# Heads' products regrouped (values with the forget gate, queries with z), and keys and values of two blocks turned by VectorE and a trip through DRAM

## The chip, the cores and the metric

The kernel runs on one core of one Trainium2 chip. A core has a matrix engine (TensorE, PE in the profile), a vector engine (VectorE, DVE), an activation engine (ScalarE, ACT), a general engine (GpSimd, POOL) and a synchronising engine (SyncE, SP), each with an instruction stream of its own that it works off in order, and 16 DMA engines that SyncE's and GpSimd's queues feed. The metric is the device time of one execution in microseconds; the kernel before took 2583.63 us, the median of three runs (2581.27 to 2584.62).

## The reference, cut to what matters

One encoder layer over 2048 prompt tokens and 64 sample tokens with 1024 features, in fp32. All projections come from one normed input `h`; the change concerns branch B, a gated linear recurrence over 8 heads with 128 features each, in chunks of 64 tokens:

```
proj = h @ w_in
vA, bA, cA, zA, q, f, iv, zB, gA, gB = split_cols(proj)
fg   = lb + (1 - lb) * sigmoid(f);   logf = log(fg);   k = 1 - fg
q    = silu(q) * 128 ** -0.5;        v = iv
# per chunk, S being the state of the head
b    = cumsum(logf);  ref = b[31]
att  = tril((q * exp(b - ref)) @ (k * exp(ref - b)).T)
o    = att @ v + (q * exp(b)) @ S
S    = exp(b_last) * S + (k * exp(b_last - b)).T @ v
yB   = (rms_norm(o) * g_onorm * silu(zB)) @ w_b_out
```

## The kernel before, in words

**Blocks.** The 2112 tokens (1408 prompt, 64 sample, 640 prompt) run as three blocks of 768, 704 and 640 tokens. Features lie on the partitions, tokens along the free axis. A block goes through branch B (`path_b`, 8 heads one after the other), branch A, the gates, the merge and the output. A block's tokens fall into groups of 128, which are pairs of chunks: six in the first block, five and the sample's lone 64 tokens in the second, five in the third. `bl["parts"]` cuts these into the first four pairs, the remaining pairs, and the lone chunk.

**Products.** Each projection is split into a high and a low fp32r part, three matmuls for one. `sgroup(i1, i2, ...)` makes two projections of the block at once from seven products (Strassen's scheme over two halves of the tokens and of the features) of twelve matmuls each (L442, L443, L444; four steps of k, three parts). The results leave in a fixed order: the first projection's first half at the fifth product, both halves of the second projection at the sixth, the first projection's second half at the seventh (with `free` the very last one goes behind the seventh). A sink takes each piece from PSUM.

**A head.** `head_prep` runs two such groups, forget gate with queries, then z with values. `scaled` runs in the middle of the second group (behind its third product) and makes, on ScalarE and VectorE, the decays `eq`, the scaled keys `kb` (`ka` for the first chunk of a pair) and the head's factors `f`; `queries` scales the queries (`qe`, and `qx` for the state). `sink_v` writes the values `vt`.

**Attention.** `head_attn` is a generator of four steps per part: (1) turn keys and values into tokens on partitions (L1068, L1070, transposes on PE into PSUM, then the copies L1072 and L1073 by ScalarE), then the scores (L1083, L1084) and their mask; (2) the state products (L1098) and the chain of states on VectorE (L1115); (3) the outputs (L1138, L1140) and their norm, whose power runs on GpSimd (L689); (4) turn the outputs back (L1156) and gate them (L1158).

**What sets the order.** Behind every product `hook()` takes the next entry of a list, so a head's attention is worked off between the products of the next head; `path_b` fills the list, step by step, part by part, and the PE instructions of a step are put behind the last product's (`placed()`). `path_b` also puts the store of a head's result (`keep_z`) and the pieces of `lead_sums` into it. A scheduler orders the other engines' streams by dependencies. Weights come through SyncE's queue, other loads and the stores through GpSimd's.

Of the kernel before, what the change touches and what calls it, by code (L numbers as in the profile page):

```python
# [18 lines left out]
P = 128  # L19
# [74 lines left out]
def hybrid_step(  # L94
# [156 lines left out]
    def used_later(idx, part):  # L251
# [5 lines left out]
        if idx in (GB * 8 + KB - 1, QQ * 8):  # L257
            return part != 0
# [677 lines left out]
    def head_prep(bl, hc, hd, first, hs):  # L936
        n, npair = bl["n"], bl["npair"]
        nch, np1 = n // CH, npair * P
        sf, qe = rt(), rt()
        sq = None if first else rt()  # L940

        def sink_f(c, h, x, y):
            if c == 0:
                A.activation(half(sf, h), whole(x, y), AF.Sigmoid)
            else:
                into(half(qe, h), x, y)

        if hs and hd == 0:
            plain_group(FF * 8, QQ * 8, hs, sink_f)
        else:  # L950
            sgroup(FF * 8 + hd, QQ * 8 + hd, hc, sink_f, first)
        if not first:
            A.activation(sq, qe, AF.Sigmoid)
        lg, b, eq = rt(), rt(), rt()
        A.activation(lg, sf, AF.Ln, bias=lb[:, hd : hd + 1], scale=omlb[:, hd : hd + 1])
        if not first:
            V.scalar_tensor_tensor(qe, qe, QK_SCALE, sq, ALU.mult, ALU.mult)
# [6 lines left out]
        ka, kb, qx, vt, z = hf(npair * CH), rt(), rt(), rt(), rt()  # L964

        late = first and hd > 0

        def scaled(after):
# [28 lines left out]
            for lo, hi in ((0, SWAP), (SWAP, npair)):  # L997
                seconds, place = slice(2 * lo + 1, 2 * hi, 2), slice(2 * lo + (hi > SWAP), 2 * hi, 2)
                V.tensor_tensor(chunks(kb)[:, place, :], chunks(sf)[:, seconds, :], chunks(lg)[:, seconds, :], ALU.mult)
            if nch % 2:  # L1000
# [3 lines left out]
            if not late:  # L1004
                queries()

        def queries():
# [3 lines left out]
            else:  # L1011
                V.tensor_tensor(qe, qe, eq, ALU.mult)
            V.tensor_tensor(chunks(qx), chunks(qe), f.unsqueeze(2).to_broadcast([P, nch, CH]), ALU.mult)

        def sink_v(c, h, x, y):
            if c == 1:
                n1 = 0
                if h == 0:
                    n1 = 2 * SWAP * CH
                    for odd in range(2):  # L1020
                        c3, to = (slice(o, 2 * SWAP, 2) for o in (odd, 1 - odd))
                        V.tensor_tensor(chunks(vt)[:, to, :], chunks(x[:, :n1])[:, c3, :], chunks(y[:, :n1])[:, c3, :], ALU.add)
                V.tensor_tensor(half(vt, h)[:, n1:], x[:, n1:], y[:, n1:], ALU.add)
# [7 lines left out]
        with behind_all(summed[-1] if first and hd == 0 else ()):  # L1031
            sgroup(ZB * 8 + hd, IV * 8 + hd, hc, sink_v, first, mid=scaled, free=late)
        if late:
            with tc.issue_after(freed[0]):
                queries()
        return dict(eq=eq, f=f, ka=ka, kb=kb, qe=qe, qx=qx, vt=vt, z=z, more=npair - 2 * SWAP, first=first, last=bl["last"], carry=None)
# [675 lines left out]
```

## Time and profile before

| quantity | value |
|---|---|
| median of 3 runs | 2583.63 us |
| the profiled execution, its own time | 2581.3 us |
| its span in the profile | 2579.6 us |
| PE busy, share of the span | 99% |
| VectorE, ScalarE, GpSimd busy | 67%, 59%, 14% |
| DMA, mean rate over the span | 287 GB/s |
| heads of the second block (1069 to 1350 us), period of a head | 35 us |
| heads of the third block (1870 to 2160 us), period of a head | 31 us |

Busy shares are means over stages; where PE has no gap, its instructions' distance from start to start is what they cost, not the duration of one, since they overlap. A matmul of two full fp32 operands shows as two records, a transpose or an fp32r matmul as one. "us to landing" of a DMA runs from its issue to the arrival of its data.

### The profile page before, as it was taken

The page shows a single profiled execution, that of the slowest core. Times are in us where ns is not written, and L with a number is a line of the kernel's source. Part 1 is how long each engine was busy: PE and PEld are TensorE (multiplying, and loading weights), DVE is VectorE, ACT ScalarE, POOL GpSimd, SP SyncE. Part 2 cuts the span into 40 slices and gives each one's busy share as a digit, 9 for nine tenths or more (in the row PEclk, how much of TensorE's full clock was granted, in tenths as well). Part 3 has the DMA queues.
Part 4 walks back from the last instruction along what each step waited for, and adds up shares of the span by engine and source line. Part 5 has one row for each costly group of instructions (what it writes and reads, how often), then busy time and mean ns, then how long its engine had stood idle before and what let it go on. Part 6 is the DMA issues. An engine that isn't in the chain of part 4 may idle for free.

```text
span 2579.6 us, 47382 instructions
## 1 busy us (share of the span) xinstructions
PE 2562.4 (99%) x16358; PEld 2546.4 (99%) x16358; DVE 1733.2 (67%) x3511; ACT 1529.9 (59%) x2973; POOL 369.5 (14%) x677
## 2 busy tenths in 40 slices
PE   9999999999999999999999999999999999999999
PEld 9999999999999999999999999999999999999998
DVE  7788778898777775466464556987345545336967
ACT  6766676454453764466564555567456665446675
POOL 2011111230022021111111221102100000001011
PEclk9999999999999999999999999999999999999999
DMA  8678777899897898877778998989887788999986
GB/s 327 225 262 289 266 258 272 314 374 304 261 348 241 267 329 264 284 249 233 261 226 290 344 392 312 325 292 338 294 271 246 251 270 265 298 297 324 334 274 201
DMA packets 361233, 739.87 MB, mean 287 GB/s; under 512 B 44118, under 2 KB 48784, under 8 KB 360992
## 3 DMA queue, kind: packets, MB, share of 16 engines
q1 hardware_dynamic: 321696, 582.69, 67.4%
q0 software_dynamic: 39296, 154.14, 16.4%
q8 instruction: 129, 2.11, 0.3%
q14 instruction: 112, 0.92, 0.1%
HBM read 543.44 MB, written 193.22 MB: 286 GB/s over the span
## 4 chain that ended last, share of the span: by engine, by line
PE 86%; issue 5%; DVE 4%; DMA 3%; ACT 1%; POOL 1%; SPq 0%; DVEq 0%; POOLq 0%; ACTq 0%
PE pg L442 18%; PE pg L443 18%; PE pg L444 18%; PE pg L594 4%; PE pg L593 4%; PE pg L595 4%; PE pg L633 3%; PE pg L632 3%; PE pg L631 3%; PE pa L1098 1%; PE pa L1138 1%; PE pa L1140 1%; PE pa L1084 1%; DMA lo<-low 1%; DVE lo L226 1%
## 5 line engine op out<-in xcount | busy, mean ns | idle before, releaser
L442 PE MATMUL pg<-r,hi 128*128 128x320 f32 (+2 forms) x3304 | 1085.2, 328 | 0.6 <-DVE r L490 0.4
L443 PE MATMUL pg<-r,hi 128*128 128x320 f32 (+2 forms) x3304 | 1068.1, 323 | 0.0
L444 PE MATMUL pg<-r,lo 128*128 128x384 f32 (+2 forms) x2356 | 768.7, 326 | 0.9 <-DMA lo<-low 0.9
L273 ACT CAST hi<-raw 128x512 fp32r<-128x512 f32 x730 | 449.6, 620 | 499.7 <-PE pg L443 172.1
L442 PEld LDWEIGHTS pg<-r,hi 128*128 128x128 f32 x3304 | 621.5, 188 | 1.9 <-issue 0.7
L443 PEld LDWEIGHTS pg<-r,hi 128*128 128x128 f32 x3304 | 621.7, 188 | 0.0
L444 PEld LDWEIGHTS pg<-r,lo 128*128 128x128 f32 x2356 | 442.3, 188 | 1.9 <-DMA lo<-low 1.7
L444 PE MATMUL pg<-r,s 128*128 128x352 f32 (+1 forms) x948 | 299.7, 316 | 0.2 <-DMA s<-low 0.2
L594 PE MATMUL pg<-r,hi 128*128 128x320 f32 (+2 forms) x864 | 277.4, 322 | 0.1
L593 PE MATMUL pg<-r,hi 128*128 128x320 f32 (+2 forms) x864 | 275.0, 322 | 0.0
L226 ACT CAST hi<-raw 128x512 fp32r<-128x512 f32 x252 | 155.5, 620 | 155.8 <-PE pg L443 40.0
L226 DVE TENSOR_TENSOR r<-r,r 128x320 fp32r<-128x320 f32 (+7 forms) x354 | 209.5, 611 | 51.9 <-ACT r L226 50.4
L226 ACT CAST r<-r 128x320 fp32r<-128x320 f32 (+7 forms) x354 | 185.8, 557 | 54.4 <-DMA r<-w_blk 10.9
L226 DVE TENSOR_TENSOR lo<-raw,hi 128x512 fp32r<-128x512 f32 x231 | 158.7, 689 | 86.8 <-ACT hi L226 81.5
L595 PE MATMUL pg<-r,lo 128*128 128x352 f32 (+2 forms) x564 | 180.8, 321 | 0.6 <-DMA lo<-low 0.6
L444 PEld LDWEIGHTS pg<-r,s 128*128 128x128 f32 x948 | 177.8, 188 | 0.7 <-DMA s<-low 0.7
L226 ACT CAST hi<-s 128x512 fp32r<-128x512 f32 x156 | 96.3, 618 | 123.9 <-PE pg L443 107.4
L632 PE MATMUL pg<-r,hi 128*128 128x384 f32 (+2 forms) x512 | 167.0, 327 | 0.2 <-DVE r L226 0.2
L631 PE MATMUL pg<-r,hi 128*128 128x384 f32 (+2 forms) x512 | 165.8, 327 | 0.2 <-ACT hi L273 0.2
L594 PEld LDWEIGHTS pg<-r,hi 128*128 128x128 f32 x864 | 162.2, 188 | 2.0 <-DVE r L226 1.4
L593 PEld LDWEIGHTS pg<-r,hi 128*128 128x128 f32 x864 | 161.3, 188 | 1.3 <-ACT r L226 0.7
L456 ACT COPY hf<-pg 128x352 f32<-128x352 f32 (+2 forms) x354 | 157.3, 446 | 1.7 <-PE pg L444 1.3
(403 smaller groups left out, 4110.9 us busy)
## 6 DMA issues: line engine op xcount, KB each, us to landing
raw<-w_blk SPq DMA_DIRECT2D x577, 256.0 KB, 4.1
raw<-S SPq DMA_DIRECT2D x444, 256.0 KB, 4.2
lo<-low SPq DMA_DIRECT2D x422, 256.0 KB, 4.1
s<-low SPq DMA_DIRECT2D x308, 256.0 KB, 4.0
low<-lo SPq DMA_DIRECT2D x271, 256.0 KB, 3.7
S<-s SPq DMA_DIRECT2D x152, 256.0 KB, 3.6
low<-r POOLq DMA_DIRECT2D x54, 256.0 KB, 5.0
r<-w_blk POOLq DMA_DIRECT2D x52, 256.0 KB, 6.6
```

The lines of the kernel that those rows point to most:

```text
L226: return A.copy(hi, src).ins, V.tensor_tensor(lo, src, hi.bitcast(F32), ALU.subtract).ins
L273: A.copy(hi, raw)
L442: add(hi[:, k, :], xhi, start=start and k == 0, stop=False)
L443: add(hi[:, k, :], xlo, start=False, stop=False)
L444: last[0] = add(lo[:, k, :], xhi, start=False, stop=k == KH - 1).ins
L456: copied = A.copy(got[n], ps[bank])
L593: add(hi[:, k, :], xhi, start=start and k == 0, stop=False)
L594: add(hi[:, k, :], xlo, start=False, stop=False)
L595: last[0] = add(lo[:, k, :], xhi, start=False, stop=k == KH - 1).ins
L631: T.matmul(ps, hi[:, k % 4, :], xhi[:, c], start=k == ks[0], stop=False)
L632: T.matmul(ps, hi[:, k % 4, :], xlo[:, c], start=False, stop=False)
L633: last[0] = T.matmul(ps, lo[:, k % 4, :], xhi[:, c], start=False, stop=k == ks[-1]).ins
```

## The change

**The groups of a head.** The first group of a head is now forget gate with values, the second z with queries, so values are there half a head earlier and queries half a head later. `queries` therefore runs behind the second group in all blocks, with the queries' sigmoid in it.

**Turning.** In the second and third block `turned` transposes the 640 columns of the five full groups in blocks of 32 by 32 on VectorE (values into the tile that later holds `qx`, keys into the one that held `b`) and stores the result to DRAM; `in_rows` loads it back in pieces of 160 elements (640 bytes), so that tokens lie on partitions. Keys come back with the five groups interleaved (an element every 20 bytes), values in pieces of 32. PE's transposes and ScalarE's copies of these groups are gone; the lone sample chunk and the whole first block keep them.

**Hooks.** In these blocks a head's steps start two hooks later than the head's list, the full groups' second steps stand in one hook, four behind their first steps, the third steps in one hook, two behind; the sample's steps lie in the hooks between. In the first block one empty hook stands ahead of each head.

```diff
             return part in ("S1", "S2", "S3", "S4")
-        if idx in (GB * 8 + KB - 1, QQ * 8):
+        if idx in (GB * 8 + KB - 1, IV * 8):
             return part != 0
...
         nch, np1 = n // CH, npair * P
-        sf, qe = rt(), rt()
-        sq = None if first else rt()
+        sf, vt = rt(), rt()
...
                 A.activation(half(sf, h), whole(x, y), AF.Sigmoid)
-            else:
-                into(half(qe, h), x, y)
+                return
+            n1 = 0
+            if h == 0:
+                n1 = 2 * SWAP * CH
+                for odd in range(2):
+                    c3, to = (slice(o, 2 * SWAP, 2) for o in (odd, 1 - odd))
+                    into(chunks(vt)[:, to, :], chunks(x[:, :n1])[:, c3, :], None if y is None else chunks(y[:, :n1])[:, c3, :])
+            into(half(vt, h)[:, n1:], x[:, n1:], None if y is None else y[:, n1:])
         if hs and hd == 0:
-            plain_group(FF * 8, QQ * 8, hs, sink_f)
+            plain_group(FF * 8, IV * 8, hs, sink_f)
         else:
-            sgroup(FF * 8 + hd, QQ * 8 + hd, hc, sink_f, first)
-        if not first:
-            A.activation(sq, qe, AF.Sigmoid)
-        lg, b, eq = rt(), rt(), rt()
+            sgroup(FF * 8 + hd, IV * 8 + hd, hc, sink_f, first)
+        lg, b, eq, qx = rt(), rt(), rt(), rt()
+        wrote = None if first else [turned("tv", vt, qx, npair)]
         A.activation(lg, sf, AF.Ln, bias=lb[:, hd : hd + 1], scale=omlb[:, hd : hd + 1])
         if not first:
-            V.scalar_tensor_tensor(qe, qe, QK_SCALE, sq, ALU.mult, ALU.mult)
             V.tensor_scalar(sf, sf, nomlb[:, hd : hd + 1], omlb[:, hd : hd + 1], ALU.mult, ALU.add)
...
         f, r = qc[:, 0, :nch], qc[:, 1, :nch]
-        ka, kb, qx, vt, z = hf(npair * CH), rt(), rt(), rt(), rt()
-        late = first and hd > 0
+        ka, kb, qe, z = hf(npair * CH), rt(), rt(), rt()
...
                 V.tensor_tensor(chunks(kb)[:, place, :], chunks(sf)[:, seconds, :], chunks(lg)[:, seconds, :], ALU.mult)
+            if not first:
+                wrote.append(turned("tk", kb, b, npair))
             if nch % 2:
...
             V.tensor_tensor(f2, f2, f1, ALU.mult)
-            if not late:
-                queries()
...
             else:
+                sq = rt()
+                A.activation(sq, qe, AF.Sigmoid)
+                V.scalar_tensor_tensor(qe, qe, QK_SCALE, sq, ALU.mult, ALU.mult)
                 V.tensor_tensor(qe, qe, eq, ALU.mult)
...
-        def sink_v(c, h, x, y):
+        def sink_q(c, h, x, y):
             if c == 1:
-                n1 = 0
-                if h == 0:
-                    n1 = 2 * SWAP * CH
-                    for odd in range(2):
-                        c3, to = (slice(o, 2 * SWAP, 2) for o in (odd, 1 - odd))
-                        V.tensor_tensor(chunks(vt)[:, to, :], chunks(x[:, :n1])[:, c3, :], chunks(y[:, :n1])[:, c3, :], ALU.add)
-                V.tensor_tensor(half(vt, h)[:, n1:], x[:, n1:], y[:, n1:], ALU.add)
+                into(half(qe, h), x, y)
             elif first:
...
         with behind_all(summed[-1] if first and hd == 0 else ()):
-            sgroup(ZB * 8 + hd, IV * 8 + hd, hc, sink_v, first, mid=scaled, free=late)
-        if late:
-            with tc.issue_after(freed[0]):
-                queries()
-        return dict(eq=eq, f=f, ka=ka, kb=kb, qe=qe, qx=qx, vt=vt, z=z, more=npair - 2 * SWAP, first=first, last=bl["last"], carry=None)
+            sgroup(ZB * 8 + hd, QQ * 8 + hd, hc, sink_q, first, mid=scaled, free=first)
+        with tc.issue_after(freed[0]) if first else nullcontext():
+            queries()
+        by_token = None
+        if not first:
+            with behind_all([*wrote, *powers]):
+                by_token = [in_rows(kind, npair) for kind in ("tv", "tk")][::-1]
+        return dict(
+            eq=eq, f=f, ka=ka, kb=kb, qe=qe, qx=qx, vt=vt, z=z, by_token=by_token,
+            more=npair - 2 * SWAP, first=first, last=bl["last"], carry=None,
+        )
...
         return t[:, : nt * P].rearrange("p (g c) -> p g c", c=P)
+    turning = {}
+    def turned(kind, src, out, npair):
+        n = npair * P
+        blocks4 = out[:, :n].rearrange("p (j a g) -> p g j a" if kind == "tk" else "p (j g a) -> p g j a", j=4, a=32)
+        V.transpose(blocks4, src[:, :n].rearrange("p (g b j) -> p g j b", b=32, j=4))
+        turning[kind] = dram.tile([P, n], F32, tag=f"{kind}{npair}", name=nm(kind), bufs=2)
+        return G.dma_start(turning[kind], out[:, :n]).ins
+    def in_rows(kind, npair):
+        t = rt(npair * P)
+        G.dma_start(t.rearrange("q (i c) -> q i c", i=4), turning[kind].rearrange("(i b) (j c) -> (b j) i c", i=4, j=4))
+        return t.rearrange("q (k g) -> q g k", g=npair) if kind == "tk" else t.rearrange("q (i g a) -> q g i a", i=4, a=32)
...
-        p_k, p_v = ps_attn(), ps_attn()
-        with placed():
-            for i, g in enumerate(gs):
-                T.transpose(p_k[:, i * P : i * P + P], cols(d["kb"], g), ident)
-            for i, g in enumerate(gs):
-                T.transpose(p_v[:, i * P : i * P + P], cols(d["vt"], g), ident)
-        kt, v = tile3(0), tile3(1)
-        A.copy(kt[rows], cols3(p_k, nt)[rows])
-        A.copy(v[rows], cols3(p_v, nt)[rows])
+        if d["by_token"] is not None and not single:
+            kt, v = (t[:, o0 // P : o0 // P + nt] for t in d["by_token"])
+        else:
+            p_k, p_v = ps_attn(), ps_attn()
+            with placed():
+                for i, g in enumerate(gs):
+                    T.transpose(p_k[:, i * P : i * P + P], cols(d["kb"], g), ident)
+                for i, g in enumerate(gs):
+                    T.transpose(p_v[:, i * P : i * P + P], cols(d["vt"], g), ident)
+            kt, v = tile3(0), tile3(1)
+            A.copy(kt[rows], cols3(p_k, nt)[rows])
+            A.copy(v[rows], cols3(p_v, nt)[rows])
         p_a = ps_attn()
...
             for i in range(nt):
-                T.matmul(p_u[:, i * P : i * P + P], kt[:, i, :], v[:, i, :], start=True, stop=True)
+                T.matmul(p_u[:, i * P : i * P + P], kt[:, i], v[:, i], start=True, stop=True)
         ss = tile3()
...
                 dst = p_o[:, i * P : i * P + P]
-                T.matmul(dst, att[:, i, :], v[:, i, :], start=True, stop=prevs[i] is None)
+                T.matmul(dst, att[:, i, :], v[:, i], start=True, stop=prevs[i] is None)
                 if prevs[i] is not None:
...
+    def each(steps):
+        for step in steps:
+            step()
     def path_b(bl, hc, first, kept, fills, hs, lead_sums=None):
...
             attn = [head_attn(i, gs, d, hd) for i, gs in enumerate(bl["parts"])]
-            hooks.extend([None] * (2 * lead))
-            for step in range(4):
+            hooks.extend([None] * (1 + lead if first else 2))
+            if not first:
+                pairs, one = attn[:2], attn[2:]
+                piece = lead_sums and [partial(next, lead_sums, None)]
+                for steps in (pairs[:1], pairs[1:], one, one, pairs, one, pairs, piece, one, pairs[:1], pairs[1:]):
+                    hooks.append(partial(each, [s if callable(s) else partial(next, s) for s in steps]) if steps else None)
+            for step in range(4 * first):
                 hooks.extend(partial(next, g) for g in attn)
                 hooks.extend([None] * (0 if step == 3 else 3 - len(attn) - (lead and step == 0) + (step == 2)))
-                if lead_sums is not None and not first and step == 2:
-                    hooks[-1] = partial(next, lead_sums, None)
             hooks.append(partial(keep_z, hd, d["z"]))
...
```

**How the instructions stand, before and after.** Three places in the third block. First PE, from the end of a head's products into the attention of that head; `pa` is attention's PSUM, `pg` the products', `hf` and `r` are tiles in SBUF. Before:

```order
L444 MATMUL pg_23801<-r_21479,lo_23762 128x320
L1068 MATMUL pa_23816<-ident,r_23588 128x128 x4
L1070 MATMUL pa_23817<-ident,r_23590 128x128 x4
L1083 MATMUL pa_23830<-r_23431,hf_23587 128x2x64
L1084 MATMUL pa_23830<-r_23431,r_23588 128x64
L1083 MATMUL pa_23830<-r_23431,hf_23587 128x2x64
L1084 MATMUL pa_23830<-r_23431,r_23588 128x64 x3
L442 MATMUL pg_23839<-r_20945,hi_23767 128x320
```

and now the same step:

```order
L444 MATMUL pg_23744<-r_21437,lo_23687 128x320
L1106 MATMUL pa_23759<-r_23496,hf_23494 128x2x64
L1107 MATMUL pa_23759<-r_23496,r_23495 128x64
L1106 MATMUL pa_23759<-r_23496,hf_23494 128x2x64
L1107 MATMUL pa_23759<-r_23496,r_23495 128x64 x3
L442 MATMUL pg_23768<-r_20853,hi_23692 128x320
L443 MATMUL pg_23768<-r_20854,hi_23692 128x320
L444 MATMUL pg_23768<-r_20853,s_23693 128x320
```

and four products further on, the state products of all five groups:

```order
L442 MATMUL pg_23744<-r_21483,hi_23710 128x320
L443 MATMUL pg_23744<-r_21484,hi_23710 128x320
L444 MATMUL pg_23744<-r_21483,lo_23711 128x320
L1121 MATMUL pa_23831<-r_23666,r_23668 128x128 x4
L1121 MATMUL pa_23841<-r_23666,r_23668 128x128
L442 MATMUL pg_23906<-r_20792,hi_23866 128x320
```

The transposes are gone, the scores open the step, and the state products read the loaded tiles `r_23666` and `r_23668` directly, in one bunch.

Second VectorE, at the end of a head, from the last of the scaled keys on. Before:

```order
L999 TENSOR_TENSOR r_23982<-r_23756,r_23972 128x3x64
L1003 TENSOR_TENSOR qc_23980<-qc_23980 128x5
L462 TENSOR_TENSOR hf_24041<-hf_24041,pg_24099 128x320
L1013 TENSOR_TENSOR r_23983<-r_23757,qc_23980 128x640
L1158 SCALAR_TENSOR_TENSOR r_23591<-pa_24113,vec,r_23591 128x512
L1158 SCALAR_TENSOR_TENSOR r_23591<-pa_24133,vec,r_23591 128x128
L1022 TENSOR_TENSOR r_23984<-hf_24041,pg_24053 128x2x64
L1029 TENSOR_TENSOR r_23985<-pg_24028,r_23985 128x320
```

and now:

```order
L1000 TENSOR_TENSOR r_23861<-r_23670,r_23848 128x3x64
L1006 TENSOR_TENSOR qc_23859<-qc_23859 128x5
L1051 STREAM_TRANSPOSE r_23849<-r_23861 128x5x128
L1181 SCALAR_TENSOR_TENSOR r_23497<-pa_24022,vec,r_23497 128x512
L490 TENSOR_TENSOR r_23862<-hf_23919,hf_23934 128x320
L1027 TENSOR_TENSOR r_23863<-pg_23906,r_23863 128x320
L490 TENSOR_TENSOR r_23862<-hf_23919,pg_23921 128x320
L1181 SCALAR_TENSOR_TENSOR r_23497<-pa_24043,vec,r_23497 128x128
L1015 SCALAR_TENSOR_TENSOR r_23862<-r_23862,r_24064 128x640
L483 TENSOR_TENSOR hf_24058<-hf_23919,pg_23962 128x320
L1016 TENSOR_TENSOR r_23862<-r_23862,r_23850 128x640
```

The keys' transpose (L1051) follows the keys at once, and the queries' chain (L490 twice, L1015, L1016), which stood earlier in the head, now closes it.

Third GpSimd's queue over one head, with the stores and loads it issues (`ms` are the norms' powers, `o` the head's result, `hgrn_p` the final state). Before:

```order
L1129 DMA hgrn_p<-state_23922 128x128
L689 TENSOR_TENSOR ms_23965<-ms_23965,mhalf 128x4
L689 TENSOR_TENSOR ms_24047<-ms_24047,mhalf 128x1
L1166 DMA o_24153<-r_23591 128x640
L1129 DMA hgrn_p<-state_24337 128x128
```

and now:

```order
L1053 DMA tv_23853<-r_23851 128x640
L1152 DMA hgrn_p<-state_23845 128x128
L689 TENSOR_TENSOR ms_23946<-ms_23946,mhalf 128x4
L689 TENSOR_TENSOR ms_23956<-ms_23956,mhalf 128x1
L1053 DMA tk_23991<-r_23849 128x640
L1058 DMA r_24069<-tv_23853 128x4x160
L1193 DMA o_24062<-r_23497 128x640
L1058 DMA r_24071<-tk_23991 128x4x160
```

Two stores and two loads came in; the keys' load stands last, behind the store of the head before, and the next head's value store stands behind it.

## The prediction

> **What bounds the kernel now.** I read the page's first part, then its chain of waits, then the busy time of two stretches: the heads of the second block (1069 to 1350 us) and of the third (1870 to 2160 us), the only places where the change takes work away.
>
> ```profile
> span 2579.6 us, 47382 instructions
> PE 2562.4 (99%) x16358; PEld 2546.4 (99%) x16358; DVE 1733.2 (67%) x3511; ACT 1529.9 (59%) x2973; POOL 369.5 (14%) x677
> PE 86%; issue 5%; DVE 4%; DMA 3%; ACT 1%; POOL 1%; SPq 0%; DVEq 0%; POOLq 0%; ACTq 0%
> ```
>
> ```profile
> 1069.00:1350.00 281.00, 281.00 (x1912) 280.07 (x1911) 167.34 (x444) 180.96 (x334) 34.65 (x58) 1.00 0.75 243
> 1350.00:1560.00 210.00, 210.00 (x1317) 209.55 (x1316) 106.63 (x214) 112.85 (x229) 47.40 (x104) 1.00 0.95 339
> 1870.00:2160.00 290.00, 290.00 (x2083) 289.78 (x2082) 154.55 (x394) 182.44 (x335) 24.64 (x40) 1.00 0.80 259
> ```
>
> The columns after the length are the busy times of PE, its weight loads, VectorE, ScalarE and GpSimd, then the clock, the DMA share and GB/s. TensorE never pauses in either stretch of heads, at the full clock (1.00), while VectorE and ScalarE are busy for 53 to 64% of them. So a PE instruction taken out there shortens the run by its pace, and nothing else does, unless the change makes PE wait.
>
> **What leaves PE.** Keys and values of the full groups of tokens are no longer turned by PE. A "mean ns of one" is no price here, since matmuls overlap; the price is the distance from start to start, in PE's instructions in order of time:
>
> ```profile
> L1070 PE MATMUL pa<-ident,r 128*128 128x128 f32 x136 | 24.0, 272 | 0.0
> L1068 PE MATMUL pa<-ident,r 128*128 128x128 f32 x136 | 23.9, 272 | 0.0
> ```
>
> ```profile
> 1084.57 0.32 PE L443 MATMUL pg<-r,hi 128*128 128x352 f32 x1
> 1084.72 0.33 PE L444 MATMUL pg<-r,lo 128*128 128x352 f32 x1
> 1084.89 0.60 PE L1068 MATMUL pa<-ident,r 128*128 128x128 f32 x4
> 1085.32 0.60 PE L1070 MATMUL pa<-ident,r 128*128 128x128 f32 x4
> 1085.76 0.39 PE L1083 MATMUL pa<-r,hf 128*128 128x128 f32 x2
> ...
> 1086.43 0.78 PE L1084 MATMUL pa<-r,r 128*128 128x64 f32 x6
> 1087.02 0.41 PE L442 MATMUL pg<-r,hi 128*128 128x352 f32 x1
> 1087.27 0.32 PE L443 MATMUL pg<-r,hi 128*128 128x352 f32 x1
> 1087.43 0.33 PE L444 MATMUL pg<-r,s 128*128 128x352 f32 x1
> ```
>
> Eight transposes take 1084.89 to 1085.76, 0.87 us, or 0.109 us each. Of the 272 that the two rows count, 10 per head in two blocks go: 10 x 8 x 2 = 160. **160 x 0.109 = 17.4 us.** The first product's matmul behind a bunch of attention work takes 1087.02 to 1087.27, 0.25 us, where its neighbours take 0.16: an interruption costs 0.09. The new hooks run the full groups' second and third steps together, which makes two interruptions fewer a head, 32 in all (the order has 225 changes from attention back to products, it had 257): **32 x 0.09 = 2.9 us.** ScalarE also loses four copies a head; it is not the bound, so that is nothing. The first block keeps its PE work: all 32 lie in the other two.
>
> **What becomes slower on PE.** In the state products (L1098, L1121 now) the turned keys are the weights, and a group's elements stand five apart, 20 bytes; values are read in pieces of 32 in a row. No row of this trace shows weights with a stride.
>
> ```profile
> 1094.01 1.05 PE L1098 MATMUL pa<-r,r 128*128 128x128 f32 x8
> 1094.82 0.41 PE L442 MATMUL pg<-r,hi 128*128 128x352 f32 x1
> ```
>
> ```profile
> L1068 PEld LDWEIGHTS pa<-ident,r x136: 137/140/146, 97.0 to 2147.9; 128*128 128x128 f32 x136
> L1098 PEld LDWEIGHTS pa<-r,r x224: 187/192/192, 104.6 to 2152.9; 128*128 128x128 f32 x112
> ```
>
> Four state products are eight records in 0.81 us, 0.10 each. L1084 above moves only 64 columns and keeps the same pace (six in 0.59 us, 0.098), so at these sizes the pace is that of the weight load, and a slower load would show. The change has 5 x 16 state products, 160 loads. Lower end: 0, since loads of 140 and 192 ns run at one pace, so some lengthening is hidden. Upper end: every load takes twice its 0.10 us, 160 x 0.10 = 16 us. A gain I exclude: the same loads, none shorter. **I take 6 us**, nearer the lower end, as the two rows of loads show about 50 ns going unseen.
>
> [...]
>
> **What must hide: the round trip.** Keys go through a VectorE transpose, a store of 327 KB, a load that GpSimd's queue issues only when the store has landed, and then the state products. When are the keys ready, and when are they wanted? In the third block before:
>
> ```profile
> 1951.92 0.39 PE L442 MATMUL pg<-r,hi 128*128 128x320 f32 x1
> 1953.77 0.38 PE L1098 MATMUL pa<-one,one 128*128 128x128 f32 x2
> ...
> 1974.40 0.60 PE L1068 MATMUL pa<-ident,r 128*128 128x128 f32 x4
> ```
>
> ```profile
> 1960.77 0.83 DVE L957 SCALAR_TENSOR_TENSOR r<-r,r 128x640 f32<-128x640 f32 x1
> 1963.95 1.48 DVE L959 TENSOR_TENSOR_SCAN r<-keep,r 128x640 f32<-128x640 f32 x1
> ...
> 1968.34 0.82 DVE L1012 TENSOR_TENSOR r<-r,r 128x640 f32<-128x640 f32 x1
> ...
> 1970.36 0.35 DVE L999 TENSOR_TENSOR r<-r,r 128x192 f32<-128x192 f32 x1
> ```
>
> ```profile
> r<-w_blk POOLq DMA_DIRECT2D x52, 256.0 KB, 6.6
> o<-r POOLq DMA_DIRECT2D x7, 352.0 KB, 4.3
> o<-r POOLq DMA_DIRECT2D x7, 320.0 KB, 5.7
> 1118.67 0.54 POOL L1166 DMA_DIRECT2D o<-r  x1 [4.28 <-DVE r L1158]
> ```
>
> Keys were complete at 1970.7; without L1012's 0.82 ahead of them and with a transpose of 0.82 (an ordinary pass over 640 columns) to 1.48 us (the scan, the slowest pass there), they are turned at 1970.7 to 1971.4. The first bunch stood behind the next head's first product, at 1974.40. The state products now stand six products later: a product is 1951.92 to 1953.77 less the 0.09, 1.76 us; the score matmuls in between are 1087.02 - 1085.76 = 1.26 for four groups and a quarter of that for the fifth, with 0.09 for each bunch, 1.8. So they come at 1974.40 + 10.6 + 1.8 = 1986.8, at least 15.4 us after the turn. The trip: 5.7 (a store of this size in this stretch) + 6.6 (the load from DRAM on this queue) + two issues of 0.54 = 13.4. It fits by 2 us. In the second block a product is 12 x 0.161 = 1.93 us and the sample's two bunches lie in between too, so the window is some 18 us, and the store took 4.3: it fits by 6. Values are turned half a head earlier. **Charge: 0.** Without that cover every us counts eight times a block.
>
> What the waiting load holds up on GpSimd's queue: the next head's value store and the powers of the norm, wanted more than half a head later. The traffic is 4 x 327 KB = 1.31 MB a head, 38 GB/s more over 35 us; the share of 0.75 and 0.80 rises towards 0.87, and the rows above show PE without a pause at 0.95.
>
> **What must hide: queries.** They now come out of a head's second group, so their sigmoid (0.76 us), L957's pass (0.83), L1012's (0.82) and two additions of 0.49 stand between the last but one product and the scores, which the two extra empty hooks put behind the third product of the next head. From that product's end to the scores lie four products, 7.0 us in the third block and 7.7 in the second. The five passes are 3.4 us; in between VectorE also has the gating of z (L1029, 0.49 twice) and the end of the head before (L1158, 1.01), 2.0 us in the third block, and with two transposes (1.6 to 3.0 us) in a head's VectorE work against none removed, it is near. Bounds: 0 to 1 us late a head, 0 to 16 us. **I take 0**, since VectorE was busy for 53 and 60% of these stretches and takes some 3 us in 31 to 35 more.
>
> ```profile
> L953 ACT ACTIVATE r<-r x16: 730/760/796, 1068.2 to 2129.7; 128x704 f32<-128x704 f32 x8, 128x640 f32<-128x640 f32 x8
> 1955.95 0.49 DVE L490 TENSOR_TENSOR r<-hf,pg 128x320 f32<-128x320 f32 x1 [0.81 <-PE pg L444]
> ...
> 1971.83 1.01 DVE L1158 SCALAR_TENSOR_TENSOR r<-pa,vec,r 128x512 f32<-128x512 f32 x2
> ...
> 1972.94 0.49 DVE L1029 TENSOR_TENSOR r<-pg,r 128x320 f32<-128x320 f32 x1
> ```
>
> **Sum.** The profiled execution took 2581.3 us (1.7 around its span). 2581.3 - 17.4 - 2.9 + 6 = 2567.0. The median of the three runs, 2583.63, lies 2.3 higher: **2569.3 us.** What a measurement can tell from no change here is about 0.2%, 5.2 us: faster is below 2578.4, slower above 2588.8.
>
> **The rivals.**
>
> *Strided weights at full price* (0.17). The 160 loads cost 16 us, and the change pays back most of what it saves: 2583.6 - 20.3 + 16 = 2579, just about no change. For it: these loads set their own pace. Against it: about 50 ns of a load was seen to go unnoticed. [...]
>
> *Keys come late* (0.12), the slower side. If loads and stores on GpSimd's queue take half as long again as their medians, which pieces of 640 bytes in place of whole rows could do, the trip in the third block is 1.5 x 12.3 + 1.1 = 19.6 us, 4.2 us too long in each of eight heads, 34 us; the second block's, 1.5 x 10.9 + 1.1 = 17.5, still fits. 2569 + 34 = 2603. It decides from a trip of 15.4 us on. Against it: both medians were taken in this traffic.
>
> *Queries come late* (0.13). VectorE's transposes run at the scan's pace or slower and push the queries a us past the scores: 2569 + 16 = 2585, no change. Against it: the VectorE time left over.
>
> *The change does not do what it says* (0.03). PE's work shrinks and the stretch doesn't, since weights arrive no faster with 38 GB/s more on the DMA engines: 2584. Against it: the stretch at 0.95.
>
> **How the numbers follow.** The forecast has 0.55, with a range of its own of 2560 (loads free, a little less) to 2578. With the strided loads at full price and late queries the range reaches 2587; below, free loads give 2563, and slightly shorter bunches 2558. That leaves late keys and half of the last rival out: 2558 to 2587. Faster: 0.55, 0.08 of the strided loads (they need not all be dear), 0.03 of the queries: 0.66. Slower: late keys 0.11, queries 0.05, the last 0.01: 0.17. No change: the rest, 0.17.
>
> **What would show it.** Right: 160 fewer transposes, PE without idle time in both stretches, each head shorter by 0.9 us. State products that run at 0.10 a record would make the time 2563; at 0.20, 2579. Wrong: idle time of PE in front of L1121 with a DMA as its releaser (keys late), or in front of L1106 or L1107 with VectorE (queries late); either would show as a wait of the same length in all heads of a block.

## The result, and the profile after

| | time, us (median, range, runs) | ratio to before, 95% interval |
|---|---|---|
| before | 2585.98 (2581.27 to 2591.01, 19) | |
| the change | 2582.64 (2577.96 to 2588.02, 19) | 0.9989 (0.9982 to 0.9996) |

The change gains 3 us, which lies within the 0.2% called no change; 2569 was predicted, the range of 2558 to 2587 holds it, because it takes in strided loads at their full price with late queries. Its profiled execution took 2583.43 us. These lines of its page answer to those of before:

```profile
span 2581.7 us, 47221 instructions
PE 2562.9 (99%) x16198; PEld 2548.5 (99%) x16198; DVE 1770.1 (69%) x3541; ACT 1491.8 (58%) x2896; POOL 407.0 (16%) x741
PE 90%; issue 3%; DVE 3%; DMA 2%; ACT 1%; POOL 0%; SPq 0%; DVEq 0%; POOLq 0%; ACTq 0%
```

PE has 160 records fewer, as counted, and is as busy as before (2562.4 us). So the work left is slower. The two stretches of heads by windows (columns as in the prediction):

```profile
1069.00:1350.00 281.00, 279.57 (x1818) 278.68 (x1817) 184.02 (x454) 170.33 (x302) 55.27 (x89) 0.99 0.82 275
1870.00:2160.00 290.00, 290.00 (x2002) 289.91 (x2001) 169.88 (x403) 172.94 (x304) 44.99 (x70) 1.00 0.86 293
```

Here are 94 and 81 records fewer in the same time: where before had 1912 matmuls, 1818 fill the stretch. Only in the second block does PE miss 1.43 us. The slower work shows in PE's order of time, at the ten records of five state products, and in the weight loads of that line:

```profile
1135.35 2.34 PE L1121 MATMUL pa<-r,r 128*128 128x128 f32 x10
1137.45 0.41 PE L442 MATMUL pg<-r,hi 128*128 128x352 f32 x1
```

```profile
L1121 PEld LDWEIGHTS pa<-r,r x256: 187/314/321, 103.4 to 2161.2; 128*128 128x128 f32 x128
```

Ten records take 2.10 us, 0.21 each, where before took 0.10; the median load (the second of the three durations) went from 192 to 314 ns, while the shortest ones, of the first block without a step, still take 187.

The second difference inside the heads stands in one place, the second head of the second block. PE waits for the queries' product; VectorE, in front of that product, for a load of weights; GpSimd, in front of that load, for VectorE's transpose, because the keys' store stands there:

```profile
1123.53 0.46 PE L1106 MATMUL pa<-r,hf 128*128 128x128 f32 x2 [1.43 <-DVE r L1016]
...
1125.28 0.49 PE L444 MATMUL pg<-r,s 128*128 128x352 f32 x1
1125.58 0.49 PE L442 MATMUL pg<-r,hi 128*128 128x352 f32 x1
```

```profile
1120.02 0.88 DVE L1015 SCALAR_TENSOR_TENSOR r<-r,r 128x704 f32<-128x704 f32 x1
1121.89 0.69 DVE L390 TENSOR_TENSOR r<-r,r 128x512 f32<-128x512 f32 x1 [0.99 <-DMA r<-w_blk]
1122.50 0.88 DVE L1016 TENSOR_TENSOR r<-r,r 128x704 f32<-128x704 f32 x1
```

```profile
1109.47 1.67 POOL L379 DMA_DIRECT2D r<-w_blk  x3
1115.25 0.55 POOL L1053 DMA_DIRECT2D tk<-r  x1 [4.12 <-DVE r L1051]
1115.79 0.54 POOL L379 DMA_DIRECT2D r<-w_blk  x1
```

Behind the wait the matmuls start 0.30 us apart instead of 0.16. The window there shows why: a granted clock of 0.66 over 5 us, that is 3.4 us at half speed (5 x 0.34 / 0.5), which costs 1.7 us more.

```profile
1125.00:1130.00 5.00, 5.00 (x24) 5.00 (x24) 1.60 (x4) 0.62 (x1) 0.00 (x0) 0.66 0.92 314
```

The round trip itself kept near the estimates; the transposes came close to the upper end (1.38 us of 0.82 to 1.48):

```profile
L1051 DVE STREAM_TRANSPOSE r<-r x32: 1319/1380/1464, 1066.6 to 2143.3; 128x640 f32<-128x640 f32 x32
tv<-r POOLq DMA_DIRECT2D x16, 320.0 KB, 3.2
tk<-r POOLq DMA_DIRECT2D x16, 320.0 KB, 4.6
r<-tv POOLq DMA_DIRECT2D x16, 320.0 KB, 6.6
r<-tk POOLq DMA_DIRECT2D x16, 320.0 KB, 6.8
```

**By stretches.** All kernels below issue the 14,298 matmuls into the products' PSUM (`pg`) in the same number and, but for some 60 records, in the same order. The start of the n-th of them can therefore be set against that of the n-th in before's profiled execution. The table gives how much longer (+) or shorter each stretch is, in us; a stretch is named by its times in before.

| stretch of before | before again | regroup | change | values_only | keys_only | pairs | rows | store_behind |
|---|---|---|---|---|---|---|---|---|
| 0 to 850 (first block) | +2.6 | -3.0 | -4.0 | -4.1 | -3.1 | -4.6 | -4.0 | -3.9 |
| 850 to 1050 | +0.1 | +2.6 | +2.1 | -0.2 | +0.1 | +2.7 | +1.6 | +3.0 |
| **1050 to 1400 (heads, second block)** | 0.0 | +0.2 | +3.1 | -4.2 | +8.2 | -8.2 | -7.5 | -0.2 |
| 1400 to 1890 | +0.4 | -0.2 | +1.8 | +0.1 | -1.0 | +4.2 | +1.8 | +3.3 |
| **1890 to 2200 (heads, third block)** | 0.0 | 0.0 | -0.3 | -4.3 | +4.3 | -5.1 | -2.0 | -0.1 |
| 2200 to the end | +0.6 | +0.1 | -0.7 | -0.5 | +0.3 | -0.4 | -0.4 | -0.5 |

Two executions of before agree to 0.0 us in both stretches of heads, so these can be read to a tenth. Outside of them, waits for single loads of weights come and go by up to 3 us. In regroup, the change, pairs and store_behind, the stretch from 850 to 1050 has such a wait of 2.3 to 2.6 us. In the change a granted clock of 0.50 follows it, from 934.10 to 937.51 us; over the whole span the clock was 0.998 there and 0.999 in the other three. rows has a wait of 2.7 us and 1.000 over its span.

### The profile page after: what moved, and what is told of

Same layout as the page of the kernel before. It is cut to its first block, busy times and chain, and to the rows that moved or that the text cites. A ratio compares the mean times of both kernels' runs of the same rounds, so it can differ in the third digit from the quotient of the medians.

```text
span 2581.7 us, 47221 instructions
## 1 busy us (share of the span) xinstructions
PE 2562.9 (99%) x16198; PEld 2548.5 (99%) x16198; DVE 1770.1 (69%) x3541; ACT 1491.8 (58%) x2896; POOL 407.0 (16%) x741
## 4 chain that ended last, share of the span: by engine, by line
PE 90%; issue 3%; DVE 3%; DMA 2%; ACT 1%; POOL 0%; SPq 0%; DVEq 0%; POOLq 0%; ACTq 0%
PE pg L442 19%; PE pg L444 19%; PE pg L443 19%; PE pg L594 4%; PE pg L593 4%; PE pg L595 4%; PE pg L633 3%; PE pg L632 3%; PE pg L631 3%; PE pa L1121 2%; PE pa L1161 1%; PE pa L1163 1%; PE pa L1107 1%; DMA raw<-w_blk 1%; PE pa L1106 1%
## 5 line engine op out<-in xcount | busy, mean ns | idle before, releaser
L444 PE MATMUL pg<-r,lo 128*128 128x384 f32 (+2 forms) x2356 | 768.4, 326 | 2.3 <-DMA lo<-low 2.3
L444 PEld LDWEIGHTS pg<-r,lo 128*128 128x128 f32 x2356 | 442.9, 188 | 3.2 <-DMA lo<-low 3.2
L444 PE MATMUL pg<-r,s 128*128 128x352 f32 (+1 forms) x948 | 300.6, 317 | 1.7 <-DMA s<-low 1.7
L444 PEld LDWEIGHTS pg<-r,s 128*128 128x128 f32 x948 | 178.5, 188 | 2.5 <-DMA s<-low 2.4
```

The lines of the kernel that those rows point to most:

```text
L444: last[0] = add(lo[:, k, :], xhi, start=False, stop=k == KH - 1).ins
```

## The experiments

**1 and 2. What a step costs TensorE.** From the kernel before, ScalarE's copy of the turned keys (scan_weights) or values (scan_moving) out of PSUM writes them with a step that differs by head; nothing else changes. In theory 1 of the first scan the step sets the pace of the loads: 0.21 us a record at 20 bytes, as in the change, against 0.10 without a step.

```diff
+        far = 1 if d["first"] or single else (6, 5, 6, 5, 1, 1, 1, 1)[hd] if d["last"] else (1, 1, 2, 2, 3, 3, 4, 4)[hd]
...
+                t = rt(far * P).rearrange("q (k g) -> q g k", g=far)[:, : min(far, nt - i)]
+                A.copy(t, cols3(p_k, nt)[:, i : min(i + far, nt)])
```

> The kernel before (PE still turns keys and values), but ScalarE's copy writes the turned keys with a stride between elements: second block heads 0-1 stride 1 (4 bytes), 2-3 stride 2, 4-5 stride 3, 6-7 stride 4 (16 bytes); third block heads 0 and 2 stride 6, heads 1 and 3 stride 5 (20 bytes), 4-7 stride 1. Only the weights of the state products (L1098) see it. [...] Theory 2 (the lost time has nothing to do with the stride): 0.10 us at all strides. Total time: theory 1 at most 5 us over the kernel before, theory 2 none.

> As the scan of the keys, but it is the values, the moving operand of the state products and of the outputs, that are written with the strides 1, 2, 3, 4, 5 and 6 in the same heads. Theory 1: the moving side has slack at 128 columns, since the pace is the weight load's (0.10 us a record, also for 64 columns), so a stride may go unseen up to twice its time; a record stays at 0.10 to 0.11 us at small strides and at most 0.11 at 5 and 6. Theory 2: no difference at any stride.

In scan_weights, eight records of state products in order of time, from their start to the next product's, at steps of 1, 2, 3, 4 and 5 elements:

```profile
1097.70 1.05 PE L1108 MATMUL pa<-r,r 128*128 128x128 f32 x8
1098.51 0.41 PE L442 MATMUL pg<-r,hi 128*128 128x352 f32 x1
...
1167.86 1.09 PE L1108 MATMUL pa<-r,r 128*128 128x128 f32 x8
1168.71 0.41 PE L442 MATMUL pg<-r,hi 128*128 128x352 f32 x1
...
1238.16 1.51 PE L1108 MATMUL pa<-r,r 128*128 128x128 f32 x8
1239.43 0.41 PE L442 MATMUL pg<-r,hi 128*128 128x352 f32 x1
...
1322.92 1.98 PE L1108 MATMUL pa<-r,r 128*128 128x128 f32 x8
1324.65 0.41 PE L442 MATMUL pg<-r,hi 128*128 128x352 f32 x1
...
1961.91 1.90 PE L1108 MATMUL pa<-r,r 128*128 128x128 f32 x8
1963.57 0.39 PE L442 MATMUL pg<-r,hi 128*128 128x320 f32 x1
```

| us a record, step | 1 | 2 | 3 | 4 | 5 | 6 |
|---|---|---|---|---|---|---|
| keys, the weights | 0.101 | 0.106 | 0.159 | 0.216 | 0.207 | 0.208 |
| values, the moving operand | 0.101 | 0.103 | 0.154 | 0.202 | 0.206 | 0.203 |

A step of eight bytes was almost free (0.106 and 0.103 us), 12 cost half as much again (0.159 and 0.154), 16 to 24 doubled the record (0.202 to 0.216). The change's own bunches, with 20 bytes, took 0.209 a record, which gives the price: 160 x (0.209 - 0.101) = 17.3 us. My expectation for values was wrong: the moving operand paid nearly the same, 0.202 to 0.206 us from 16 bytes on. The whole times, one execution each, were 2595.4 us, 10 above before's median where I had expected 5 at most, and 2605.4 (values with a step go into the output products too).

**3 and 4. Half the trip.** Values alone go through DRAM, or keys alone; PE turns the other.

```diff
-                by_token = [in_rows(kind, npair) for kind in ("tv", "tk")][::-1]
+                by_token = [in_rows("tv", npair)]
```

> The changed kernel with the trip for values alone: PE turns the keys again in all blocks, so the state products' weights are contiguous. Theory 1 (the keys' strided weights cost 17 us): 80 transposes fewer, 8.7 us, and 32 interruptions fewer, 2.9, against the kernel before: ratio 0.9955 (about 11.6 us less). Theory 2 (the trip itself, its traffic, the later queries or VectorE eat the gain): about half of the gain and half of the loss, ratio 0.998 to 1.000.

> The changed kernel with the trip for keys alone: PE turns the values again. Theory 1: 8.7 us of transposes and 2.9 of interruptions saved, 17.4 us paid for 160 strided weight loads: 5.8 us slower than before, ratio 1.0022. Theory 2: as values alone, ratio 0.998 to 1.000.

values_only: 2570.85 us, ratio 0.9943 (0.9931 to 0.9956); keys_only: 2590.25, 1.0022 (1.0012 to 1.0033). Both ratios came out as expected, but partly by luck: the expectations counted 2.9 us for interruptions, and run 5 shows none of it in the heads; the first block made up for it. In the table the values' trip saves 4.2 and 4.3 us in the stretches of heads (80 transposes x 0.109 / 2 = 4.36 a block), and the keys' trip costs 4.3 in the third block, 80 x 0.108 = 8.64 for the loads less 4.36. In the second it costs 8.2, with a wait of 1.9 us on the queries in the same place as the change; the granted clock was 0.99 from 1069 to 1350 us, as in the change.

**5. The regrouping alone.** No trip; new order of products and hooks.

```diff
-        wrote = None if first else [turned("tv", vt, qx, npair)]
...
-                wrote.append(turned("tk", kb, b, npair))
```

> The heads' products regrouped and the queries' chain behind the second bunch, as in the change, but no round trip: PE turns keys and values as before, 16,358 matmul records. The theory (the change gained 17.4 us by the 160 transposes and lost 17.4 us to the loads of strided keys at twice the pace, so that what is left of it is the regrouping with its fewer interruptions): 2.9 us less than before, ratio 0.9989, which is the change's own. Rival (the regrouping costs, by queries that are late, and the trip gained a little): ratio 1.000 to 1.003, with a PE wait on the queries' products on VectorE in several heads.

2579.33 us, 0.9978 (0.9969 to 0.9987): a little more than I expected, and from another place. In the heads of blocks two and three it gains nothing (+0.2, 0.0). Saving the interruptions gains nothing. In before, eight state products and, further on, the two of the one-group part:

```profile
1129.06 1.05 PE L1098 MATMUL pa<-r,r 128*128 128x128 f32 x8
1129.87 0.41 PE L442 MATMUL pg<-r,hi 128*128 128x352 f32 x1
1130.11 0.33 PE L443 MATMUL pg<-r,hi 128*128 128x352 f32 x1
...
1131.88 0.38 PE L1098 MATMUL pa<-one,one 128*128 128x128 f32 x2
1132.02 0.41 PE L442 MATMUL pg<-r,hi 128*128 128x352 f32 x1
1132.27 0.32 PE L443 MATMUL pg<-r,hi 128*128 128x352 f32 x1
```

and in regroup, in one bunch:

```profile
1099.59 1.05 PE L1115 MATMUL pa<-r,r 128*128 128x128 f32 x8
1100.48 0.39 PE L1115 MATMUL pa<-one,one 128*128 128x128 f32 x2
1100.62 0.41 PE L442 MATMUL pg<-r,hi 128*128 128x352 f32 x1
1100.87 0.32 PE L443 MATMUL pg<-r,hi 128*128 128x352 f32 x1
```

Apart: 0.81 + 0.14, and 0.24 + 0.25 for the two products' matmuls behind instead of 0.16 each, 1.12 us in all. Together: 1.03 + 0.25 - 0.16 = 1.12. The 0.08 is paid between the two parts inside the bunch as well. What the regrouping does gain lies in the first block, 2.8 us between 100 and 500 us of before, to 0.01 us the same in every kernel that has it. Before's waits of PE have a row there that the others lack:

```profile
PE pa L1083 <- DVE att L1092: 1.3, 2, 0.8
```

With those waits two bunches of twelve records took 2.43 and 2.24 us, without them 1.42, so they account for 1.8 us of the 2.8. Most likely the extra empty hook gives VectorE a product more to finish the copies on which they wait; the hook was not tried alone.

**6 and 7. Keys without the step.** pairs lays two groups beside each other, a step of 8 bytes; rows has the load put the keys in order, in pieces of 128 bytes, without a step.

```diff
-        blocks4 = out[:, :n].rearrange("p (j a g) -> p g j a" if kind == "tk" else "p (j g a) -> p g j a", j=4, a=32)
+        blocks4 = out[:, :n].rearrange("p (j g a) -> p g j a", j=4, a=32)
...
+                t.rearrange("q (g i a) -> q g i a", i=4, a=32),
+                turning[kind].rearrange("(i b) (j g a) -> (b j) g i a", i=4, j=4, a=32),
```

(that of rows; that of pairs has three turns with 256-byte pieces.)

> The change, with the keys laid out two groups to a pair in the DRAM buffer, so that a state product's keys come with a step of 2 elements (8 bytes) where the change has 16 or 20 bytes; three turns on VectorE take the place of one for the keys, and the buffer has 768 columns for five groups. The theory: a step of 8 bytes loads at 0.106 us a record where 16 bytes took 0.21, so 160 products take some 16.6 us less than in the change; less what the longer trip of the keys costs (about 0.5 to 1 us of VectorE and of DMA more, against 2.5 us of slack): 2,565 to 2,568 us on the chip where before takes 2,586, ratio 0.992 to 0.993 with 0.21 to 0.22 for a pair of records in the state products. Rival (the state products are slow because of where the tile comes from, the DRAM round trip, and not because of the step): 0.21 a record as in the change, ratio 0.999.

> The change, with the keys laid out in the DRAM buffer as the values are and put in order by the load back, in pieces of 128 bytes (2,048 or 2,560 of them where the change has 512): the keys of a state product lie in one row, without a step. The theory: state products at 0.10 us a record, 17.4 us less than the change, and from that what the load of small pieces is late by. The change's load landed in 6.7 us with 2.5 us to spare; if it lands in 9 us or less nothing is lost, ratio 0.992; if it takes 12 us, 3 us in each of 16 heads are lost, 48 us, ratio 1.011, with a wait of the state products on a DMA in each head. The keys' slack in the third block decides between them; the pace of the products is 0.10 in either.

pairs: 2570.1 us, 0.9938 (0.9925 to 0.9950); rows: 2568.15, 0.9936 (0.9923 to 0.9948). The loads of their state products, and what then came late, with the landing of rows' load of keys:

```profile
L1139 PEld LDWEIGHTS pa<-r,r x256: 187/196/197, 103.5 to 2147.4; 128*128 128x128 f32 x128
PE pa L1139 <- DMA r<-tk: 1.6, 2, 1.2
```

```profile
L1127 PEld LDWEIGHTS pa<-r,r x256: 186/192/193, 104.0 to 2148.4; 128*128 128x128 f32 x128
PE pa L1127 <- DMA r<-tk: 5.3, 6, 1.6
r<-tk POOLq DMA_DIRECT2D x16, 320.0 KB, 9.2
```

196 and 192 ns in place of 314: the step was the cost, not the trip. Both kernels stay a little short of the 0.992 expected. In the second block pairs wins 8.2 us of the 8.7 that its 80 transposes cost; in the third, where the change's load landed only 0.9 to 2.9 us ahead of the state products in seven heads, keys come late: rows' load takes 2.4 us longer than the change's, by the medians.

**8 to 11. Moving hooks, and before a second time.** piece_last runs line 390's piece behind the heads' transposes; pairs_later and rows_later do too, and have state and output products of the third block a product later.

```diff
-                for steps in (pairs[:1], pairs[1:], one, one, pairs, one, pairs, piece, one, pairs[:1], pairs[1:]):
+                order = (pairs[:1], pairs[1:], one, one, pairs, one, pairs, one, pairs[:1], pairs[1:], piece)
+                if not one:
+                    order = (pairs[:1], pairs[1:], one, one, one, pairs, one, pairs, one, pairs[:1], pairs[1:])
```

> The change, with one hook of the second block moved: the piece of the layer's sums of weights (line 390) runs behind the heads' last transposes, and the output products of the single-group part take its place, so that VectorE no longer has a piece that waits for its weights ahead of the queries' products. Theory (of the trip, nothing is left in the sum but the stall: transposes out, strided weights in, both 17.4 us; the stall of 1.43 us and the half clock behind it, 1.7 us, are the 3 us by which the change is slower than the regrouping alone): no PE wait on L1016, 3.1 us less than the change, ratio to before 0.9977, the same as the regrouping alone. Rival (the stall was not on the path, what the trip costs is elsewhere): ratio 0.9989 as the change, with the same stall-free PE.

> The kernel with keys in pairs of groups, and in the third block the state products and the output products one product (1.76 us) later; the piece of line 390 last, as in piece_last. In the pairs kernel the third block gained 5.1 us where two steps of 8 bytes should have given 8.3, with keys up to 1.2 us late in three heads. Theory (the keys were late by less than one product): no wait on the keys, 3.2 us less than the pairs kernel, ratio 0.9925. Rival (the later outputs make the heads' ends late, since the norm's chain now has one product less): a PE wait at the transposes behind it in eight heads, 0.994 or more.

> The kernel with the keys put in order by the load, with the same two moves of hooks. In the rows kernel the keys were late in six heads by 5.3 us in all, 1.6 us at most, and the two blocks gained 9.5 us where 17.4 were to be had. Theory (products without a step at 0.101 us a record, keys no longer late): some 7 us less than the rows kernel, ratio 0.991, and the fastest of all. Rival (the clock, half for 3.4 us behind each wait, or the later outputs eat it): 0.9935 as the rows kernel.

> The kernel before, a second time, as a control: ratio 1.000 within its interval. The first profile of before was among its fastest executions (2,581.3 us where the median of 19 is 2,586.0), so this one should show some 3 us of waits of PE that the first one lacks; if they stand at loads of weights (line 444 or 595 on a DMA) with half the clock behind them, the medians differ from the profiles by chance waits outside the heads; if none is seen, that difference stays open.

All three moves lost against the kernels that they start from: 1.0007 (0.9999 to 1.0016), 1.0064 (1.0048 to 1.0080), 1.0047 (1.0033 to 1.0061). PE's waits in piece_last, then in rows_later:

```profile
PE pa L1093 <- DVE att L1115: 2.9, 1, 2.9
```

```profile
PE pa L1185 <- DVE r L1180: 18.5, 7, 2.7
```

In piece_last the wait for the load now stands in front of the scores' copies, and lasts longer (5.81 us of VectorE, 0.99 in the change). In the other two the keys are in time, but the outputs' norm, with a product less, is late for the transposes in seven heads. before_again came to 1.0000 (0.9991 to 1.0009); its profile is 3.7 us longer than the first, none of it in the heads. Among its waits of PE at L444 are these on weights, where the first profile has 0.9 us on such a load and none on a split:

```profile
PE pg L444 <- DVE lo L226: 1.8, 2, 1.2
PE pg L444 <- DMA lo<-low: 2.1, 2, 1.8
```

**12 to 14. The store, and the state products alone.** store_behind hands the keys' store to GpSimd's queue after the head's second group; rows_both and pairs_both do that and have only the state products of the third block a product later.

```diff
-                wrote.append(turned("tk", kb, b, npair))
+                turned("tk", kb, b, npair)
...
+        if not first:
+            wrote.append(stored("tk", b, npair))
```

> The change, with the keys' store handed to GpSimd's queue behind the head's second group instead of in the middle of it. It moves one row of that queue: the fourth load of line 379 in the second block's second head no longer stands behind a store that waits 4.1 us for VectorE's transpose. Theory (that store is what made the load late, the load made line 390 late on VectorE, that the queries' products, and these PE: 1.43 us of wait and 1.7 us of half clock): no PE wait on L1016, the heads of the second block 3.0 us shorter than in the change, the third block's the same to 0.1 us, and the second block's heads within 0.1 us of the regrouping alone. Rival (the wait moves on, as in piece_last): another PE wait of 1 us or more at the head of that bunch and the heads as long as in the change.

> The rows kernel (keys without a step) with the keys' store behind the second group, and in the third block the state products alone one product later, the outputs where they were. Theory: no wait on the keys, 17.4 us less in the two blocks' heads than in the regrouping alone, some 7 us less than the rows kernel: 2,561 us where before takes 2,585, ratio 0.991. Rival (VectorE's states, some 2 us behind the state products, now come too late for the outputs one product of 1.76 us later): a PE wait at the outputs in eight heads of the third block, 4 us or more with the clock behind it, ratio 0.9935 or above.

> The pairs kernel (keys with a step of 8 bytes) with the same two moves. Theory: no wait on the keys, 0.106 us a record in the state products against 0.101: 1 us more than the rows kernel with both, 2,562 us, ratio 0.9915. Rival: as for that kernel, a PE wait at the outputs of the third block, ratio 0.9935 or above.

GpSimd's order in store_behind, and the wait of PE that rows_both has in exchange:

```profile
1110.35 2.19 POOL L379 DMA_DIRECT2D r<-w_blk  x4
1116.14 0.55 POOL L1060 DMA_DIRECT2D tk<-r  x1 [3.59 <-DVE r L1053]
```

```profile
PE pa L1176 <- DVE r L1151: 2.8, 6, 0.8
```

The wait on L1016 is gone, and the second block's heads are 3.3 us shorter than the change's (-0.2 against +3.1), the third's the same (-0.1 against -0.3). So the place of the store caused the wait. How much went by way of the load is shown in part only: in the change's trace VectorE stood idle for 0.99 us on it, of PE's 1.43; and with the store moved, the scheduler also put three of line 390's four passes behind L1016, where in the change all four stand ahead. The whole time doesn't show it: 2581.98 us, 0.9990 (0.9980 to 1.0000), an interval of 5 us. rows_both (2569.58, 0.9939, 0.9926 to 0.9951) and pairs_both (2573.39, 0.9956, 0.9942 to 0.9970) gain nothing on rows and pairs. The rival was right in kind: VectorE's states come late for the outputs, in rows_both by up to 0.8 us in six heads, 2.8 us in all where it named eight heads and 4 us.

values_only, pairs, rows and rows_both are 14 to 17 us faster than before, pairs_both 10.6. The first four can't be told apart, and values_only is the simplest of them.

## Why the prediction was wrong

- **Transposes, 17.4 us: right.** values_only shows 4.2 and 4.3 us for 40 of them.
- **Strided weights, "I take 6 us": the step that failed.** It was 17.3, just above the upper end of 16, and so 11.3 of the 14.3 us that I forecast as a gain did not come. That upper end, a load at twice its time, was my estimate: no run had shown a load with a step by then. scan_weights showed 0.207 to 0.216 us a record from a step of 16 bytes on, for 0.101 without. I reasoned that loads of 140 and 192 ns run at one pace, so some 50 ns of any lengthening go unseen, and stayed near the lower end. But 192 ns is the length that is already at that pace; what comes on top is paid nearly in full: 122 ns more on the load gave 108 ns more on the record. The two rows said what a shorter load gains, nothing; not what a longer one costs. The rival of full price had this mechanism, with a chance of 0.17; that its time, 2579, also lies near the 2582.6 measured is partly luck, since it still counts 2.9 us for interruptions, and leaves out the queries' wait and the first block's gain.
- **Interruptions, 2.9 us: wrong.** Regroup shows 0 in the heads; what an interruption costs is paid between the parts inside a longer bunch too.
- **First block, no effect: wrong.** 2.8 us of gain, 1.8 of them from two waits on VectorE that the new order does not have.
- **Keys' trip hidden by 2 us: right.** No wait of PE on keys, but the room was narrower in places: by the landings in the trace, seven heads of the third block had 0.9 to 2.9 us (the sixth had 14). The load below was issued at 1980.59 and landed at 1987.17, 2.6 us ahead of the state products (GpSimd's and PE's order of time):

```profile
1980.59 0.76 POOL L1058 DMA_DIRECT2D r<-tk  x1 [2.63 <-issue]
```

```profile
1989.79 1.45 PE L1121 MATMUL pa<-r,r 128*128 128x128 f32 x6
```

- **Queries, 0: wrong in one head of 16.** 1.43 us and 1.7 of half clock. The half clock is not in every execution: 6 of the change's 19 have a granted clock of 1.000 over the span, which 3.4 us at half, 1.7 of 2580, would bring down to 0.999. I named what the waiting load holds up on GpSimd's queue, but not what the waiting store does, and overlooked the loads of line 379 there. A wait in all heads, as I wrote, it was not.

The sum in the heads: -17.4 + 17.3 + 3.1 = +3.0, measured +2.9 (3.14 - 0.25). With 4.0 us less in the first block and 2.1 and 1.8 more in the two stretches outside of the heads, the change's profiled execution is 2.1 us longer than before's. Medians differ by -3.3 us, and two things stay open there. Before's usual execution is longer than its first profile, in the second one by waits for weights outside of the heads. And the stretch from 1400 to 1890 us is 0.9 to 4.7 us longer in the nine kernels that send both keys and values through DRAM, and at most 0.4 longer in regroup, values_only, keys_only and before's second profile. But the two scans, which send nothing through DRAM, are 2.1 and 2.8 longer there too, so the trip is not shown to be the cause. PE's waits in that stretch are small ones, at loads and splits of weights among others.

## What to carry to other kernels

Price the step of an operand of TensorE by a scan before trading transposes for a layout: fp32 elements 16 to 24 bytes apart doubled the record here (0.202 to 0.216 us for 0.101), 8 bytes apart were nearly free (0.103 and 0.106), and both operands paid. When a change has two halves of one kind, try each alone: values_only gains 14.6 us in the medians, both halves together 3.3. And where a store that waits for compute enters a queue in order, look for the loads behind it, and for who waits for those.

## What was not expected of the hardware

A record's time followed the step between 2 and 4 elements only. For the weights it was 0.106, 0.159 and 0.216 us at steps of 2, 3 and 4, so 0.053 and 0.057 more for an element more; a step of 2 cost 0.005 over none, and 5 and 6 took 0.207 and 0.208, no more than 4. The values went the same way: 0.103, 0.154 and 0.202, then 0.206 and 0.203. Why it stops at 4 no run shows.

In the change a wait of 1.43 us was followed by half the clock for 3.4 us (0.50 from 1125.24 to 1128.66 us). Waits of up to 1.6 us on the keys in rows, and one of 2.7 us on weights, had no such result: its granted clock stayed at 1.000 over the span. So the length of a wait alone did not decide it in these runs, and what does was not shown: no run varied that alone.
